# Up stores on ScalarE's and GpSimd's queues, fixed halo buffers, and a reordered beginning of the last projection in a hybrid decoder layer

## The chip, the cores and the metric

The kernel runs on one core of one Trainium2 chip. The metric is the device time in microseconds of one execution; the median of three runs of the kernel before is 2043.06 us (2043.0 to 2047.3). All arithmetic is float32; every matrix product is made of three passes (high part by high part, high by low, low by high), with a float32 split into a part that TensorE takes as it is (float32r) and the rest.

## The reference

One layer: a gated pair of token mixers, a projection with a layer norm, and then a gated feed-forward block with a three-tap causal convolution over time, again with a layer norm. The change touches the feed-forward block only (1024 positions, width 1024, hidden width 2816, so 5632 up columns):

```python
def conv_ffn(h, w_up, dw_w, dw_b, w_down):
    u = causal_dwconv(h @ w_up, dw_w, dw_b)
    gate, val = jnp.split(u, 2, axis=-1)
    return (jax.nn.silu(gate) * val) @ w_down

...
        ffn = conv_ffn(h, w_ffn_up[l], ffn_dw_w[l], ffn_dw_b[l], w_ffn_down[l])
        h = layer_norm(DN_ALPHA * h + ffn, ln2_g[l], ln2_b[l])
```

## The kernel before, in words

Both products of the feed-forward block are computed by a scheme of seven block products in place of eight: the operands are cut into 2 x 2 blocks, sums and differences of blocks are formed by VectorE, seven products are made, and their results are combined.

**Before the feed-forward block** (`ffn_blocks`, line 735): the normalised rows are transposed by TensorE, and the blocks b11, b21 (tile h1b1), b22, t1, t2 (tiles h1s) and t3, t4 (tile h1b2) are split into high and low parts. The pool of this stage is closed before the pool `up` opens, so that tiles of `up` stand in its memory.

**Up projection, first part** (`up_first`, line 806): for the first eight (`LEAD`) of 22 column blocks j the two products that need only b11 and b21 are made early, beside the transposing. ScalarE copies the bank (line 814), and a DMA on SyncE's queue (SP) stores the copy to `first_scr` (line 815).

**Up projection, rest** (`up_rest`, line 837): for each j, `up_weights` (line 817) loads two weight tiles `ra` (pool `wst`, tag `st`, three buffers, shared with all other weight loads) and `rb` (pool `up`, tag `raw`, three buffers), VectorE forms their sums (lines 828 to 831), and ScalarE and VectorE split them (lines 731, 732). TensorE makes five products (seven from j = 8 on) of 12 matmuls each. For j < 8 the early results are loaded back from `first_scr` (lines 859, 860). VectorE combines the banks into the gate and value columns `ug`, `uv` (lines 863 to 877), in three buffers of 1056 columns whose first two are zeroed by GpSimd (lines 846, 847), as the convolution reads two columns to the left. Then follow the three taps (line 883 on ScalarE, line 887 twice on VectorE), silu and the product (lines 897, 898), in three buffers `o`. Every second j belongs to the lower half of the hidden width; there VectorE forms the sums for the next scheme of seven (lines 912 to 915). All results go to HBM by DMAs on SP's queue: lines 908, 910, 916 and 917 (`b11_scr`, `b2_scr`, `t32_scr`, `t41_scr`).

**Last projection** (`down`, line 919): seven products p = 0 to 6, each of 11 steps k, a step being 12 matmuls. `load(p, k)` (line 952) fetches the step's block x of the hidden layer (line 968) and its weight blocks (lines 970 to 991) and splits them (lines 1006, 1007). Two sums of weight blocks are kept over several products: c3 (in a tile of the pool `big`, which has two buffers and holds h1b1 and h1b2 until the up projection has read them) and c4. In p = 0 the blocks a11 and a21 are loaded and c3 = a11 + a21 is formed; in p = 1, a12 and a22 and c4 = a12 + a22; p = 2 adds c3 to a22; p = 3 takes c3 and adds it to c4; p = 6 takes c4. The eight row tiles of the residual stream (`rows`, the other buffer of `big`) are loaded at the start (line 936). After each product VectorE adds its four banks to the rows (lines 1023 to 1054), and when a row tile is complete its layer norm is taken and it is stored.

**Order**: the functions are written in program order, and a scheduler orders the instructions of each engine by priority and a modelled time line when the program is built; `tc.high_priority(offset=n)` moves weight loads and their splits up. At run time each engine and each engine's DMA queue works strictly in the order that came out: an instruction that waits holds up all that stand behind it on its queue. Tiles in the same memory wait for each other's last readers.

Of the kernel before, what the change touches and what calls it, by code (L numbers as in the profile page):

```python
# [8 lines left out]
F32 = mybir.dt.float32  # L9
# [7 lines left out]
P = 128  # L17
# [39 lines left out]
def kernel(  # L57
# [748 lines left out]
    def up_first(fp, bl, j):  # L806


        w = weights(wup[2 * j], f"ue{j}")
        ps = bank(1)  # L810
        for q, block in enumerate(("b11", "b21")):
            product(ps, lambda i: w[:, i, q * HALF : (q + 1) * HALF], bl[block], q == 0)
            f = fp.tile([P, HALF], F32, tag="first", bufs=4, name=f"first{q}_{j}")
            A.copy(f, ps)
            SY.dma_start(first_scr[j][q], f)

    def up_weights(upp, j):


        with tc.high_priority(offset=2000):  # L820
            r1 = wst.tile([P, D], F32, tag="st", name=f"ra{j}")
            SY.dma_start(r1, wup[2 * j])
            r2 = upp.tile([P, D], F32, tag="raw", bufs=3, name=f"rb{j}")
            SY.dma_start(r2, wup[2 * j + 1])
            a11, a12, a21, a22 = r1[:, :HALF], r1[:, HALF:], r2[:, :HALF], r2[:, HALF:]
            ue = None if j < LEAD else split_pair(wsp, r1, f"ue{j}")
            s3 = upp.tile([P, HALF], F32, tag="s3", name=f"s3_{j}")
            V.tensor_tensor(out=s3, in0=a11, in1=a21, op=ALU.add)
            V.tensor_tensor(out=a21, in0=a21, in1=a22, op=ALU.add)
            V.tensor_tensor(out=a11, in0=a21, in1=a11, op=ALU.add)  # L830
            V.tensor_tensor(out=a12, in0=a12, in1=a11, op=ALU.add)
            w24 = split_pair(wsp, r1, f"s24_{j}")
            w10 = split_pair(wsp, r2, f"s10_{j}")
            w3 = split_pair(upp, s3, f"s3_{j}", HALF, 2)
        return ue, w24, w10, w3

    def up_rest(upp, bl, j, before):

        ue, w24, w10, w3 = up_weights(upp, j)
        ug, uv = (
            upp.tile([P, T + 32], F32, tag="u", bufs=3, name=f"f{n}{j}") for n in ("ug", "uv")
        )
        s = upp.tile([P, HALF], F32, tag="s", bufs=2, name=f"s{j}")
        G.memset(ug[:, :2], 0.0)
        G.memset(uv[:, :2], 0.0)
        early, late = slice(2, 2 + HALF), slice(2 + HALF, 2 + T)
        ps, pz = bank(1 if ue else 0), bank(0)
        if ue:  # L850
# [54 lines left out]
        )  # L905
        early, late = slice(0, HALF), slice(HALF, T)
        if j < NK:
            SY.dma_start(b11_scr[j], ov[:, early])
            return ov
        SY.dma_start(b2_scr[j - NK], ov)  # L910
        a, b, t = before, ov, og
        V.tensor_tensor(out=t[:, early], in0=a[:, late], in1=b[:, late], op=ALU.subtract)
        V.tensor_tensor(out=a[:, late], in0=a[:, early], in1=a[:, late], op=ALU.subtract)
        V.tensor_tensor(out=t[:, late], in0=t[:, early], in1=a[:, early], op=ALU.subtract)
        V.tensor_tensor(out=a[:, early], in0=b[:, early], in1=t[:, late], op=ALU.add)
        SY.dma_start(t32_scr[j - NK], t)
        SY.dma_start(t41_scr[j - NK], a)

    def down(upp, dp, g, b):

        LAST = 8
        X, Y = [bank(1) for _ in range(4)], [bank(0) for _ in range(4)]

        def flat_big(name):
# [5 lines left out]
        c4.append(upp.tile([P, HALF], F32, tag="s3", name="c4_last"))  # L932
        rs = [rows[:, t * D : (t + 1) * D] for t in range(8)]
        sts = [dp.tile([P, 2, 6], F32, name=f"st_f{t}") for t in range(8)]
        for t in range(8):
            SY.dma_start(rs[t], h1_scr[t * P : (t + 1) * P, :])
        E, L = slice(0, HALF), slice(HALF, D)

        def add(dst, x, y):
# [12 lines left out]
        def load(p, k):  # L952

            nonlocal n_steps
            a11, a21, a12, a22 = (wdown[h * NK + k, :, cs] for h in range(2) for cs in (E, L))
            x = (
                b11_scr[k],
                b2_scr[k][:, E],
                t32_scr[k][:, L],
                t32_scr[k][:, E],  # L960
                t41_scr[k][:, L],
                t41_scr[k][:, E],
                b2_scr[k][:, L],
            )[p]
            with tc.high_priority(offset=4000):
                st = raw("dr")
                w_st = st[:, E]
                SY.dma_start(st[:, L], x)
                if p == 0:
                    SY.dma_start(w_st, a11)  # L970
                    SY.dma_start(c3[k], a21)
                    add(c3[k], c3[k], w_st)
                elif p == 1:
                    SY.dma_start(w_st, a12)
                    SY.dma_start(c4[k], a22)
                    add(c4[k], c4[k], w_st)
                elif p == 2:
                    SY.dma_start(w_st, a22)
                    add(w_st, w_st, c3[k])
                elif p == 3:  # L980
                    w_st = c3[k]
                    add(c4[k], c4[k], c3[k])
                elif p == 4:
                    other = raw("do")[:, E]
                    SY.dma_start(w_st, a21)
                    SY.dma_start(other, a22)
                    add(w_st, w_st, other)
                elif p == 5:
                    SY.dma_start(w_st, a22)
                else:  # L990
                    w_st = c4[k]
                if p == 6 and k >= NK - 4:
                    if not last:
                        last.append(big_tile("last").rearrange("p i k t -> p (i k t)"))
                    w = last[0][:, (k - NK + 4) * 2 * D : (k - NK + 5) * 2 * D]
                    w = w.rearrange("p (i n) -> p i n", i=2)
                else:
                    own = n_steps % 2 and n_steps > 2
                    w = (dp if own else wsp).tile(
                        [P, 2, D], F32R, tag="w", bufs=3, name=f"w_dn{p}_{k}"  # L1000
                    )
                cuts = ((slice(0, D), st),) if w_st is not c3[k] and w_st is not c4[k] else (
                    (E, w_st), (L, st[:, L])
                )
                for cs, src in cuts:
                    A.copy(w[:, 0, cs], src)  # L1006
                    V.tensor_tensor(  # L1007
                        out=w[:, 1, cs], in0=src, in1=w[:, 0, cs].bitcast(F32), op=ALU.subtract
                    )
            n_steps += 1  # L1010
            return w
# [53 lines left out]
        for p, (banks, first, then) in enumerate(products):  # L1065
            end = NK - LAST if p == 6 else NK
            for k in range(end):
                w = load(p, k)
                for t in range(4):
                    block(banks[t], w, t, first, k)  # L1070
            ws = {k: load(p, k) for k in range(end, NK)}
            for t in range(4):
                for k in ws:
                    block(banks[t], ws[k], t, first, k)
                then(t)
# [26 lines left out]
    with pool("firsts", side="right") as fp:  # L1102
        for j in range(LEAD):
            up_first(fp, bl, j)
    upp = ctx.enter_context(pool("up"))
    before = None
    for j in range(NF):
        before = up_rest(upp, bl, j, before)
    ffn_stack.close()
    dp = ctx.enter_context(pool("down", side="right"))  # L1110
    g, b = row(dp, RW_2G, D, "ln2_g"), row(dp, RW_2B, D, "ln2_b")
# [100 lines left out]
```

## Time and profile before

| | |
|---|---|
| median of the runs | 2043.06 us |
| the profiled execution, first to last instruction | 2043.0 us |
| up_first ends (its last matmul) | 1402.5 us |
| up_rest, j = 0 to 7 | 1412.9 to about 1544 us |
| up_rest, j = 8 to 21 | to about 1816 us |
| last projection's matmuls | about 1805 to 2033.8 us |
| last layer norms and stores | to 2043.0 us |

The profile is of one execution. Times in it are counted from the first instruction. "PE" is TensorE's matmuls, "DVE" VectorE, "ACT" ScalarE, "POOL" GpSimd, "SP" SyncE, which issues all DMAs of this kernel; SPq marks its issues. "PEclk" or the granted clock is the share of full speed that TensorE was given. A row of a waits view reads: who waited, at which line, for which instruction; us in total, times, longest. A row of a time line reads: start, duration, engine, line, operation, output <- input, and in brackets the idle time before it and what ended it. In a chain view each row is a piece of the chain that ended last: start, duration, what.

### The profile page before, as it was taken

How to read it: one execution, taken by the hardware profiler on the slowest of the kernel's cores; microseconds unless marked ns; L12 is line 12 of the kernel's file. 1: busy time of each engine (PE TensorE's matmuls, PEld its weight loads, DVE VectorE, ACT ScalarE, POOL GpSimd, SP SyncE). 2: the span in 40 equal slices, each digit the busy share in tenths (PEclk: the TensorE clock that was granted, in tenths of full speed). 3: DMA queues.
4: the chain of work that ended last, by engine and by line, in shares of the span. 5: the costliest groups of instructions: out<-in, count | busy, mean ns of one | idle time of the engine just before them, and what ended most of it. 6: DMA issues, size and time to landing. Idle time of an engine off the chain costs nothing. (4 is left out here: it accounts for less than half of the span.)

```text
span 2043.0 us, 24683 instructions
## 1 busy us (share of the span) xinstructions
PE 1977.0 (97%) x9164; PEld 1627.7 (80%) x9164; DVE 1717.1 (84%) x2279; ACT 1001.3 (49%) x1431; POOL 146.8 (7%) x125
## 2 busy tenths in 40 slices
PE   7999999999999999999999999997899999989998
PEld 6888887888788888888888888876678888768886
DVE  7599999989766859999998976596888788789668
ACT  4465654556452356665454645453334445444432
POOL 2010101000400001010100040010000000000000
PEclk9999999999999999999999999998989999999999
DMA  6212223223436522222323253564343223287463
GB/s 218 93 68 89 87 93 103 98 103 114 160 124 218 200 93 73 93 78 87 117 88 109 107 175 127 207 234 174 124 138 119 95 98 117 101 316 267 145 226 109
DMA packets 99192, 275.10 MB, mean 135 GB/s; under 512 B 11264, under 2 KB 11264, under 8 KB 99072
## 3 DMA queue, kind: packets, MB, share of 16 engines
q1 hardware_dynamic: 99072, 273.52, 38.4%
q8 instruction: 72, 1.18, 0.2%
q14 instruction: 48, 0.39, 0.1%
HBM read 223.93 MB, written 49.55 MB: 134 GB/s over the span
## 5 line engine op out<-in xcount | busy, mean ns | idle before, releaser
L420 DVE SCALAR_TENSOR_TENSOR c<-v,pc,c 128x512 f32<-128x512 f32 x480 | 374.5, 803 | 7.7 <-ACT c L409 6.4
L478 POOL TENSOR_TENSOR au<-seg_mv,head_of 128x1024 fp32r<-128x1024 f32 x32 | 76.4, 2386 | 963.0 <-PE sm L487 730.1
L166 PE MATMUL acc<-hT,w_c 128*128 128x512 f32 x352 | 141.0, 401 | 0.0
L167 PE MATMUL acc<-hT,w_c 128*128 128x512 f32 x352 | 140.6, 399 | 0.0
L168 PE MATMUL acc<-hT,w_c 128*128 128x512 f32 x352 | 138.4, 393 | 0.0
L375 DVE SCALAR_TENSOR_TENSOR xbc<-u,pc,xbc 128x512 f32<-128x512 f32 x144 | 109.6, 773 | 0.7 <-ACT xbc L373 0.5
L1006 ACT CAST w_dn<-dr 128x1024 fp32r<-128x1024 f32 (+1 forms) x73 | 68.3, 944 | 76.6 <-PE sm L168 27.4
L167 PE MATMUL acc<-w_z,hT 128*128 128x512 f32 x256 | 100.8, 394 | 0.0
L166 PE MATMUL acc<-w_z,hT 128*128 128x512 f32 x256 | 100.8, 401 | 0.0
L168 PE MATMUL acc<-w_z,hT 128*128 128x512 f32 x256 | 100.7, 396 | 0.0
L154 ACT CAST w_c<-st_c 128x1024 fp32r<-128x1024 f32 x50 | 52.6, 1051 | 86.9 <-PE acc L168 66.2
L1007 DVE TENSOR_TENSOR w_dn<-dr,w_dn 128x1024 fp32r<-128x1024 f32 (+1 forms) x73 | 78.6, 1086 | 9.3 <-ACT w_dn L1006 9.1
L167 PEld LDWEIGHTS acc<-hT,w_c 128*128 128x128 f32 x352 | 66.1, 188 | 16.9 <-issue 3.8
L168 PEld LDWEIGHTS acc<-hT,w_c 128*128 128x128 f32 x352 | 66.1, 188 | 16.1 <-issue 2.6
L166 PEld LDWEIGHTS acc<-hT,w_c 128*128 128x128 f32 x352 | 66.1, 188 | 16.0 <-issue 2.6
L155 DVE TENSOR_TENSOR w_c<-st_c,w_c 128x1024 fp32r<-128x1024 f32 x47 | 60.5, 1287 | 20.3 <-ACT w_c L154 20.3
L166 PE MATMUL acc<-h1b,w_ue 128*128 128x512 f32 x176 | 68.8, 391 | 2.6 <-ACT w_ue L731 1.4
L731 ACT CAST w_s<-rb 128x1024 fp32r<-128x1024 f32 x22 | 23.2, 1053 | 94.7 <-PE sm L168 73.1
L166 PE MATMUL sm<-h1b,w_s 128*128 128x512 f32 x176 | 69.4, 395 | 0.0
L167 PE MATMUL sm<-h1b,w_s 128*128 128x512 f32 x176 | 69.2, 393 | 0.0
L168 PE MATMUL sm<-h1b,w_s 128*128 128x512 f32 x176 | 69.0, 392 | 0.0
L167 PE MATMUL acc<-h1b,w_ue 128*128 128x512 f32 x176 | 68.5, 389 | 0.0
(348 smaller groups left out, 5859.7 us busy)
## 6 DMA issues: line engine op xcount, KB each, us to landing
st_c<-wcol SPq DMA_DIRECT2D x50, 512.0 KB, 3.5
st_z<-wz SPq DMA_DIRECT2D x32, 512.0 KB, 3.5
dr<-wdown SPq DMA_DIRECT2D x55, 256.0 KB, 4.4
st_wo<-wo SPq DMA_DIRECT2D x24, 512.0 KB, 4.1
ra<-wup SPq DMA_DIRECT2D x22, 512.0 KB, 3.5
rb<-wup SPq DMA_DIRECT2D x22, 512.0 KB, 3.5
t_scr<-fo SPq DMA_DIRECT2D x22, 512.0 KB, 4.3
dr<-t_scr SPq DMA_DIRECT2D x44, 256.0 KB, 3.2
```

Source lines behind the costliest of these rows:

```text
L154: A.copy(w[:, 0, :], st)
L155: (eng or V).tensor_tensor(out=w[:, 1, :], in0=st, in1=w[:, 0, :].bitcast(F32), op=ALU.subtract)
L166: TE.matmul(ps, wa(0), xa(0), start=start, stop=False, skip_group_check=more)
L167: TE.matmul(ps, wa(0), xa(1), start=False, stop=False, skip_group_check=more)
L168: TE.matmul(ps, wa(1), xa(0), start=False, stop=stop, skip_group_check=more)
L375: V.scalar_tensor_tensor(out=o, in0=u[:, k : k + HALF], scalar=pc[:, wc + k : wc + k + 1], in1=o, op0=ALU.mult, op1=ALU.add,)
L420: V.scalar_tensor_tensor(out=accs[i], in0=v[:, k : k + HALF], scalar=pc[:, wc + k : wc + k + 1], in1=accs[i], op0=ALU.mult, op1=ALU.add,)
L478: G.tensor_tensor(out=au, in0=seg_mv[:, c, :].unsqueeze(1).to_broadcast([P, 8, P]), in1=head_of[:, g, :].unsqueeze(2).to_broadcast([P, 8, P]),
L731: A.copy(w[:, 0, :], src)
L1006: A.copy(w[:, 0, cs], src)
L1007: V.tensor_tensor(out=w[:, 1, cs], in0=src, in1=w[:, 0, cs].bitcast(F32), op=ALU.subtract)
```

## The change

In `up_first` the store is issued by ScalarE. In `up_weights` the second weight tile of j = 0 comes from the pool `wst`. In `up_rest` the columns lie in three buffers that are allocated once and whose first two columns are zeroed once, and the stores of the results are issued by GpSimd. In `down` the row loads go to GpSimd's queue, four after step 2 of product 0 and four after step 2 of product 2; product 0 loads only a11 (for the first five steps once into the staging tile and once, by GpSimd, into c3; from then on into c3 alone), product 1 loads only a12, into c4; product 2 loads a21 and a22 and forms c3 = a11 + a21, a22 + c3, and c4 = a12 + a22 + c3. From product 3 on the same sums are used.

```diff
@@ up_first
             A.copy(f, ps)
-            SY.dma_start(first_scr[j][q], f)
+            A.dma_start(first_scr[j][q], f)
@@ up_weights
-            r2 = upp.tile([P, D], F32, tag="raw", bufs=3, name=f"rb{j}")
+            if j:
+                r2 = upp.tile([P, D], F32, tag="raw", bufs=3, name=f"rb{j}")
+            else:
+                r2 = wst.tile([P, D], F32, tag="st", name=f"rb{j}")
@@ up_rest
-        ug, uv = (
-            upp.tile([P, T + 32], F32, tag="u", bufs=3, name=f"f{n}{j}") for n in ("ug", "uv")
-        )
+        ug, uv = us[2 * j % 3], us[(2 * j + 1) % 3]
-        G.memset(ug[:, :2], 0.0)
-        G.memset(uv[:, :2], 0.0)
...
-            SY.dma_start(b11_scr[j], ov[:, early])
+            G.dma_start(b11_scr[j], ov[:, early])
-        SY.dma_start(b2_scr[j - NK], ov)
+        G.dma_start(b2_scr[j - NK], ov)
...
-        SY.dma_start(t32_scr[j - NK], t)
-        SY.dma_start(t41_scr[j - NK], a)
+        G.dma_start(t32_scr[j - NK], t)
+        G.dma_start(t41_scr[j - NK], a)
@@ down
-        LAST = 8
+        LAST, EARLY = 8, 5
-        for t in range(8):
-            SY.dma_start(rs[t], h1_scr[t * P : (t + 1) * P, :])
+        def load_rows(ts):
+            for t in ts:
+                G.dma_start(rs[t], h1_scr[t * P : (t + 1) * P, :])
@@ load
-                if p == 0:
+                if p == 0 and k < EARLY:
                     SY.dma_start(w_st, a11)
-                    SY.dma_start(c3[k], a21)
-                    add(c3[k], c3[k], w_st)
+                    G.dma_start(c3[k], a11)
+                elif p == 0:
+                    w_st = c3[k]
+                    SY.dma_start(w_st, a11)
                 elif p == 1:
+                    w_st = c4[k]
                     SY.dma_start(w_st, a12)
-                    SY.dma_start(c4[k], a22)
+                elif p == 2:
+                    other = raw("do")[:, E]
+                    SY.dma_start(other, a21)
+                    SY.dma_start(w_st, a22)
+                    add(c3[k], c3[k], other)
+                    add(w_st, w_st, c3[k])
                     add(c4[k], c4[k], w_st)
-                elif p == 2:
-                    SY.dma_start(w_st, a22)
-                    add(w_st, w_st, c3[k])
                 elif p == 3:
                     w_st = c3[k]
-                    add(c4[k], c4[k], c3[k])
@@ the loop over products
                     block(banks[t], w, t, first, k)
+                if k == 2 and p in (0, 2):
+                    load_rows(range(2 * p, 2 * p + 4))
@@ before the loop over j
+    us = [upp.tile([P, T + 32], F32, name=f"u{i}") for i in range(3)]
+    for u in us:
+        G.memset(u[:, :2], 0.0)
...
-        before = up_rest(upp, bl, j, before)
+        before = up_rest(upp, us, bl, j, before)
```

More of the change, by code (lines that the diff above doesn't have):

```diff
@@ L835, in up_weights, with up_rest @@
         return ue, w24, w10, w3
-    def up_rest(upp, bl, j, before):
+    def up_rest(upp, us, bl, j, before):
         ue, w24, w10, w3 = up_weights(upp, j)
-        ug, uv = (
-            upp.tile([P, T + 32], F32, tag="u", bufs=3, name=f"f{n}{j}") for n in ("ug", "uv")
-        )
+        ug, uv = us[2 * j % 3], us[(2 * j + 1) % 3]
         s = upp.tile([P, HALF], F32, tag="s", bufs=2, name=f"s{j}")
-        G.memset(ug[:, :2], 0.0)
-        G.memset(uv[:, :2], 0.0)
         early, late = slice(2, 2 + HALF), slice(2 + HALF, 2 + T)
```

## The prediction

> **What bounds the kernel now.** I read the page first, then busy time by stage, then PE's waits, then the time line at each gap.
>
> ```profile
> PE 1977.0 (97%) x9164; PEld 1627.7 (80%) x9164; DVE 1717.1 (84%) x2279; ACT 1001.3 (49%) x1431; POOL 146.8 (7%) x125
> ```
>
> TensorE is the bound: 97% of the span of 2043.0 us. Only what it loses can be won, so the question is where the last third, the only part the diff touches, loses time. Busy time by stretches (PE, weight loads, DVE, ACT, POOL, then granted clock, DMA share, GB/s):
>
> ```profile
> 1402.50:1412.90 10.40, 0.41 (x3) 0.01 (x1) 4.98 (x9) 2.91 (x5) 0.00 (x0) 0.69 0.73 277
> 1412.90:1544.00 131.10, 118.17 (x482) 95.28 (x483) 114.04 (x140) 45.68 (x46) 1.21 (x12) 0.93 0.38 131
> 1544.00:1809.00 265.00, 263.30 (x1159) 216.82 (x1158) 216.44 (x245) 124.41 (x149) 2.92 (x29) 1.00 0.31 111
> 1809.00:1852.00 43.00, 35.36 (x141) 27.70 (x140) 36.82 (x42) 18.86 (x20) 0.00 (x0) 0.92 1.04 387
> 1852.00:2034.00 182.00, 181.83 (x803) 150.22 (x801) 144.72 (x207) 71.08 (x93) 0.00 (x0) 1.00 0.52 177
> ```
>
> There are three holes: at 1402, between 1413 and 1544, and between 1809 and 1852. The rest has none. PE's waits from 1402 on name them:
>
> ```profile
> PE sm L166 <- DVE fuv L869: 12.3, 3, 5.2
> PE sm L166 <- ACT w_s L731: 10.6, 2, 10.0
> PE acc L166 <- ACT w_dn L1006: 4.4, 1, 4.4
> PE acc L167 <- DVE w_dn L1007: 2.5, 2, 1.3
> ```
>
> A long wait costs a second time, because the clock falls. PE's time line, a steady stretch and the one behind the first hole:
>
> ```profile
> 1393.77 0.39 PE L166 MATMUL acc<-h1b,w_ue 128*128 128x512 f32 x1
> ...
> 1398.30 0.39 PE L168 MATMUL acc<-h1b,w_ue 128*128 128x512 f32 x1
> ...
> 1412.89 0.80 PE L166 MATMUL sm<-h1s,w_s 128*128 128x512 f32 x1 [9.99 <-ACT w_s L731]
> ...
> 1416.04 0.63 PE L168 MATMUL sm<-h1b,w_s 128*128 128x512 f32 x1
> ```
>
> Twenty starts lie between the first two rows: 4.53/20 = 0.227 us each. Between the last two lie seven: 3.15/7 = 0.45 us. **Hole A** (1402) is 10.0 us of idling; nine starts at the low clock, to 1416.8, lose some 9 x 0.21 = 1.9 us more: **11.9 us**. **Hole B**: the three waits on L869 are 12.3 us, and behind the two longest (5.2 and 4.5), from 1478.8 to 1484.9 and from 1513.7 to 1519.0, 14 and 12 starts at the same slow spacing lose 26 x 0.21 = 5.5 us: **17.8 us**. **Hole C**, the beginning of the last projection: 2.5 and 4.4 us of waits, and 12 slow starts behind the longer one, from 1837.8 to 1843.1, 2.5 us: **9.4 us**. Together 39 us; PE cannot get under about 2043 - 39 = 2004 by this change.
>
> **Part 1: the stores of up_first move from SP to ACT, and the second weight tile of j=0 to the staging pool.** SP's queue at hole A, and the DVE instruction it holds up:
>
> ```profile
> 1386.62 0.33 SPq L822 DMA_DIRECT2D ra<-wup  x1
> ...
> 1394.40 9.52 SPq L815 DMA_DIRECT2D first_scr<-first  x5
> 1403.97 1.39 SPq L824 DMA_DIRECT2D rb<-wup  x3
> 1407.89 0.69 DVE L828 TENSOR_TENSOR s<-ra,rb 128x512 f32<-128x512 f32 x1 [14.57 <-DMA rb<-wup]
> ```
>
> The last stores of up_first wait in SP's queue for ScalarE's copies of the last products. Behind them stand the first three rb loads, and DVE idles 14.6 us for them. The stores now stand behind their own copies on ACT, and rb0 no longer needs memory of the transposing stage: it takes the second staging buffer, which SP refilled at 1386.6 (now with ra1). With the 3.9 us that rb took from issue to use (1403.97 to 1407.89) it is there at about 1390.5. From L828 to the first matmul took 1412.89 - 1407.89 = 5.0 us. DVE is busy with the transposing stage until 1407.89 - 14.57 = 1393.3, so the first product is ready at about 1398.5, before PE's last matmul at 1402.5. The hole closes: **-11.9 us**. What hides the 4 us of spare time is up_first's last products; next late is w10, whose buffer only opens with the release of ue6, one product earlier.
>
> ACT pays for 16 issues:
>
> ```profile
> 1320.00:1402.50 82.50, 79.73 (x376) 65.45 (x375) 65.54 (x88) 49.34 (x78) 9.94 (x9) 1.00 0.63 229
> ```
>
> One issue takes 0.33 us on SP (L822 above), so by that some 16 x 0.33 = 5.3 us on ACT, which has 33 us idle in these 82.5. Hidden, 0; if that cover were gone, PE would wait 0.3 us per copy, since each second product adds onto the bank that ACT copies first.
>
> **Part 2: fixed halo buffers.** Gone are 44 two-column memsets (1.21 + 2.92 us of POOL above, on no chain); the three buffers rotate as before. 0.
>
> **Part 3: up_rest's stores move from SP to POOL.** Chain into the second L869 wait:
>
> ```profile
> 1469.14 5.80 DMA t_scr<-fo
> ...
> 1475.02 1.16 ACT fo L883
> ...
> 1478.14 0.61 DVE fuv L869
> 1478.79 0.80 PE sm L166
> ```
>
> and ScalarE's wait of this kind between 1395 and 1560 (us in total, times, longest):
>
> ```profile
> ACT fo L883 <- DMA t_scr<-fo: 5.3, 2, 2.9
> ```
>
> ScalarE waits until a conv buffer's store has landed, DVE's L887 waits for ScalarE, and L863 and L869, which PE needs, are queued behind it on DVE. SP issued that store as soon as it was ready, so SP's queue was not the trouble here, and the other queue gains nothing. What a store costs on POOL's queue no row shows, as before has no DMA from POOL. From below it is 0, or a little under, if POOL issues as promptly as SP (0.33 us); from above it is a POOL operation over a whole tile:
>
> ```profile
> L478 POOL TENSOR_TENSOR au<-seg_mv,head_of 128x1024 fp32r<-128x1024 f32 x32 | 76.4, 2386 | 963.0 <-PE sm L487 730.1
> 1384.22 1.29 POOL L785 TENSOR_TENSOR ts<-h1raw,ts 128x512 f32<-128x512 f32 x1 [4.63 <-DVE h1s L755]
> ```
>
> I take the shorter, 1.3 us, as nearer to an instruction that touches 128 rows but not all of their data. ScalarE waits for a store twice, each time ahead of one of the two long L869 waits: **+2.6 us** (0 to +4.8). The Trainium skill weighs in against this part: "SBUF — State Buffer", section "SBUF: two separate sides", says that a DMA from GpSimd has its descriptors written by GpSimd, and that a VectorE instruction in a 2-port mode can hold them up, 620 ns becoming 3100. By that rule at its worst the term would be an estimated 2 x 2.5 = 5.0 us; but the page gives those modes to copies, casts and tensor_scalar, and VectorE's operations in the chain above are none of these. No run here shows it yet.
>
> **DVE's lead.** With PE starting at 1402.5 DVE can have worked from 1393.3, 9 us, instead of 5 us as now. In 1412.9 to 1544 DVE worked 114 of 131 us, so it is nearly the bound there, and up to 4 us of lead can come off hole B. But the buffers of the split weights let it run ahead by little more than one step. I take half: **-2 us** (0 to -4).
>
> **Part 4: the last projection.** The chain into its long wait:
>
> ```profile
> 1830.06 6.54 DMA dr<-wdown
> 1836.69 1.05 ACT w_dn L1006
> ```
>
> After ScalarE's cast PE starts, at 1837.8. The block that ScalarE waits for (dr, a step of product one) is issued only at 1830, and takes 6.5 us. DMA is full here: 387 GB/s at a share of 1.04. Ahead of it in SP's queue, from 1796 to 1827, stand the eight row loads and the burst of blocks to be kept (c); the issues by size and median time to landing:
>
> ```profile
> c<-wdown SPq DMA_DIRECT2D x21, 256.0 KB, 5.4
> rows<-h_scr SPq DMA_DIRECT2D x8, 512.0 KB, 8.1
> ```
>
> So 22 of these 256 KB loads (one goes to the tile c_last), 5.8 MB. The first two products now take 22 x's, 22 blocks and 5 extra copies, 49 loads, instead of 66: 17 x 0.262 = 4.5 MB less. Four of the row tiles (2.1 MB) can come two products later. 6.6 MB at 387 GB/s are 17 us of DMA time, more than the hole. The 4.4 us wait and its slow clock go: **-6.9 us** (0 to -9.4). I leave the 2.5 us on DVE's L1007, where DVE still has the last blocks' conv to do.
>
> The 22 moved loads and adds fall in product three. DVE's groups there:
>
> ```profile
> L1007 DVE TENSOR_TENSOR w_dn<-dr,w_dn 128x1024 fp32r<-128x1024 f32 x20 | 24.0, 1213 | 0.8 <-ACT w_dn L1006 0.8
> L940 DVE TENSOR_TENSOR dr<-dr,c 128x512 f32<-128x512 f32 x11 | 7.3, 678 | 0.0
> L1027 DVE TENSOR_TENSOR rows<-rows,sm 128x512 f32<-128x512 f32 x4 | 2.6, 674 | 0.0
> L207 DVE BATCH_NORM_STATS2 st_f<-rows 128x6 f32<-128x512 f32 x4 | 2.5, 676 | 0.0
> ```
>
> Eleven steps of 1.21 + 3 x 0.68 = 3.25 us, plus 5.1 us at its start, are 41 us, against PE's 132 x 0.227 = 30.0. At most 11 us are missing, and the products on both sides have one split per step (13.3 us of 30), so DVE can run ahead there. A step takes two staging tiles of six, so its loads lead by three steps, 8.2 us, and the weights by up to six. I take 0, up to +3.
>
> **The sum**, against the profiled execution's 2043.0, which is its span and the lower end of the runs shown (median 2043.06): 2043.0 - 11.9 + 2.6 - 2.0 - 6.9 = 2024.8 us.
>
> **Rivals.** (1) *Hole B goes too.* Its waits come from an order on DVE, and the schedule of the whole up stage is made anew. If L863 and L869 stand ahead of the conv, all 17.8 us fall: 2043.0 - 11.9 - 17.8 - 6.9 = 2006. Against it: DVE's 114 of 131 us. (2) *Only one end wins.* The 11 blocks of product two (2.9 MB, 7.5 us at 387 GB/s) and the rows still burst ahead of the steps, or product three's DVE work takes back what product one gained: 2043.0 - 11.9 + 2.6 - 2.0 = 2031.7; with hole C closed and A not, 2038.7. (3) *No change.* The queues were not what was late: rb comes in time, but another part of step 0 (its s and ug from the first_scr stores, now ACT's) or the transposing stage's memory holds PE as long. Then 2043, within 4. The Trainium skill, "DMA: Bandwidth & Descriptors", section "Issuing engines are not separate DMA queues", has a rule to this effect: several issuing engines save only the time to initiate a DMA. By it only some 16 x 0.33 = 5.3 us of SP's issue time would be freed, none of it PE's; the 9.52 us row of L815 speaks against it, as that is waiting in order, not issue. (4) *Slower.* Late stores on POOL put more conv waits ahead of L863 and L869 in the first eight steps. Such a stall costs 5.2 + 14 x 0.21 = 8.1 us; two are there now. The other terms bring 11.9 + 2.0 + 6.9 = 20.8 us, so it decides from the third additional one on: three give 2043.0 - 20.8 + 24.3 = 2046, five 2063. For it: nothing but the buffers' number (three) covers a store; against it: only the odd steps store t tiles, and half of those four stall already. From step 8 on DVE has 48.6 us idle in 265 and would absorb it.
>
> **How the numbers follow.** Forecast, 2017 to 2032: 0.51. Rival 1, 2003 to 2017: 0.17. Rival 2, 2031 to 2039: 0.17. Rival 3: 0.06. Rival 4: 0.09. Predicted 2024.8. From 2004 to 2039 lie the forecast, rival 2 and most of rival 1, a little over 0.8; the bounds of the unknown costs, +2.2 for the stores, +2 for the lead, +6.9 for hole C and +3 for product three, end at 2024.8 + 14.1 = 2038.9. A change of 0.2%, 4 us, is about what a measurement of this kernel can tell from none: faster 0.85, within it 0.06, slower 0.09.
>
> **What would show it.** Step 1: rb0 issued near 1387, DVE's first L828 before 1396, no gap over 1 us at the switch to up_rest, granted clock 1.00 there. Step 3: t_scr's time to landing, and the L869 waits. Step 4: DMA share under 1 and no wait on L1006 at the start of the last projection; PE full through product three. I am wrong if PE still idles at the switch, if more than three waits on L869 are left, or if a new wait stands on L940.

## The result and the profile after

The changed kernel takes 2038.18 us (median of ten runs, 2035.64 to 2043.9), the kernel before 2044.17 us in ten runs beside it: a ratio of 0.9973, 95% interval 0.9963 to 0.9983, or some 5.5 us less. The forecast was 18.2 us less. The sign is right and the size is not. The profiled execution of the changed kernel is the slowest of its ten (span 2042.2 us); a second profile of the same kernel was taken with the experiments. The profile of the kernel before is of a run at the fast end of its own (2043.0 against a median of 2044.17), so the two profiles differ by less than the medians.

Busy time of the changed kernel by the stretches of its holes (PE, weight loads, DVE, ACT, POOL, granted clock, DMA share, GB/s); the stretches between them are full:

```profile
1402.50:1413.40 10.90, 5.60 (x14) 4.16 (x14) 8.38 (x11) 4.85 (x6) 0.00 (x0) 0.69 0.81 271
1413.40:1544.00 130.60, 120.22 (x500) 96.36 (x500) 116.05 (x142) 46.52 (x47) 7.16 (x13) 0.96 0.37 128
...
1804.20:1850.30 46.10, 37.15 (x138) 29.54 (x137) 30.97 (x37) 20.90 (x30) 6.41 (x12) 0.85 0.82 310
```

All three holes are still there: matmuls stand in 5.6 of 10.9 us at the first, and in 37 of 46 us at the beginning of the last projection, where the clock is now lower (0.85) than before (0.92). The four largest of PE's waits from 1380 on:

```profile
PE sm L166 <- DVE u L868: 9.2, 3, 3.9
PE sm L166 <- ACT w_s L731: 6.0, 2, 5.3
PE acc L166 <- ACT u L866: 5.7, 2, 5.4
PE acc L166 <- ACT w_dn L1012: 3.5, 1, 3.5
```

The longest wait for the split weights (A) is halved, from 10.0 to 5.3 us, and not gone; the waits behind the conv (B) are 3.1 us shorter, and the last projection has two waits of 5.4 and 3.5 us where it had one of 4.4 and two of 1.3.

To compare kernels I count at each hole what PE's starts lie further apart than the 0.227 us of a steady stretch, so the slow starts behind a wait count too. "Last matmul" is where PE's list ends.

| us lost by PE | A (switch, to 1428) | B (to 1535) | C (from 1787) | last matmul |
|---|---|---|---|---|
| before | 12.0 | 19.5 | 11.4 | 2033.4 |
| changed | 7.9 | 16.0 | 14.9 | 2032.1 |
| changed, second profile | 8.0 | 13.3 | 12.5 | 2028.7 |

So the changed kernel won 4 us at A and 3.5 to 6 at B, and gave 1 to 3.5 back at C, where 6.9 were to be won. B differs by 2.7 us between two profiles of the same kernel, so a difference of that size there says little.

**At A** the loads came as predicted: rb0 is issued at 1386.65 and VectorE's first sum runs at 1393.27. VectorE's and the chain's rows:

```profile
1393.27 0.68 DVE L831 TENSOR_TENSOR s<-ra,rb 128x512 f32<-128x512 f32 x1
...
1404.61 0.69 DVE L732 TENSOR_TENSOR w_s<-s,w_s 128x512 fp32r<-128x512 f32 x1 [9.93 <-ACT w_s L731]
```

```profile
1402.98 0.59 ACT first L814
...
1403.96 0.63 ACT w_s L731
...
1408.24 0.80 PE sm L166
```

The sum was ready at 1393.95 (1393.27 + 0.68); its high part is made only at 1403.96. ScalarE works in order, and the cast stands behind the copy of up_first's last product, which ends with up_first itself. VectorE idles 9.93 us for it. In the kernel before the order was the other way round; the same cast found ScalarE idle and waited 5.04 us for VectorE's sum:

```profile
1408.62 0.62 ACT L731 CAST w_s<-s 128x512 fp32r<-128x512 f32 x1 [5.04 <-DVE s L828]
```

rb0's new place also moved another load. The staging pool has three buffers. In before they hold ra0, ra1 and ra2; in the changed kernel rb0 takes one, and ra2 leaves SyncE 18.7 us later (first row before, second row changed; ra2 is the first of its three):

```profile
1391.36 0.33 SPq L822 DMA_DIRECT2D ra<-wup  x1
```

```profile
1410.08 3.27 SPq L822 DMA_DIRECT2D ra<-wup  x3
```

**At C** there are two bursts. GpSimd's time line at the first, and what ScalarE waits for:

```profile
1791.95 2.71 POOL L973 DMA_DIRECT2D c<-wdown  x5 [17.06 <-PE acc L168]
1794.65 0.54 POOL L909 DMA_DIRECT2D b_scr<-fo  x1
...
1818.90 4.25 POOL L937 DMA_DIRECT2D rows<-h_scr  x8 [5.18 <-PE sm L168]
```

```profile
1804.35 1.15 ACT L882 ACTIVATE fo<-u,pc 128x1024 f32<-128x1024 f32 x1 [3.91 <-DMA b_scr<-fo]
1807.30 1.15 ACT L882 ACTIVATE fo<-u,pc 128x1024 f32<-128x1024 f32 x1 [1.80 <-DMA t_scr<-fo]
...
1809.39 0.56 ACT L866 COPY u<-acc 128x512 f32<-128x512 f32 x1
```

When the memory of c3 opens near 1792, five of its blocks are issued by GpSimd and six by SyncE at once. Three stores of up_rest follow them. Their landings free the conv buffers: the first tap (L882) waits for the b_scr store, the second for a t_scr store, and the copy that PE waits for (L866) is queued on ScalarE behind both. The same kinds of store in a calm stretch (1544 to 1785) and here (1785 to 1806), by count, size and median us to landing:

```profile
t_scr<-fo POOLq DMA_DIRECT2D x12, 512.0 KB, 3.8
...
b_scr<-fo POOLq DMA_DIRECT2D x6, 512.0 KB, 2.9
```

```profile
t_scr<-fo POOLq DMA_DIRECT2D x2, 512.0 KB, 12.0
...
b_scr<-fo POOLq DMA_DIRECT2D x1, 512.0 KB, 9.6
```

The second burst: all eight row tiles go together at 1818.9, among ten blocks of c4 that SyncE issues from 1815.5 to 1822.4, though four of the rows were written two products later in the program. No data that these four need holds them back to that place, and the scheduler put them together. A block of the hidden layer pays, as the chain shows:

```profile
1827.19 16.75 DMA dr<-b_scr
...
1844.63 0.79 PE acc L166
```

### The profile page after: what moved, and what is told of

The parts are those of the page before. It is cut to its first block, busy times and chain, and to the rows that moved or that the text cites. A ratio compares the mean times of both kernels' runs of the same rounds, so it can differ in the third digit from the quotient of the medians.

```text
span 2042.2 us, 24581 instructions
## 1 busy us (share of the span) xinstructions
PE 1981.6 (97%) x9164; PEld 1630.7 (80%) x9164; DVE 1712.8 (84%) x2285; ACT 1001.6 (49%) x1448; POOL 173.1 (8%) x141
## 4 chain that ended last, share of the span: by engine, by line
PE 71%; DVE 20%; DMA 4%; issue 3%; ACT 1%; SPq 0%; POOL 0%; DVEq 0%; ACTq 0%; POOLq 0%
PE acc L166 18%; PE acc L168 18%; PE acc L167 18%; DVE c L420 6%; PE sm L166 4%; PE sm L167 4%; PE sm L168 3%; PE sm L534 2%; DMA dr<-b_scr 1%; PE acc L357 1%; DVE xbc L375 1%; DVE fo L886 1%; PE sm L515 1%; PE sm L192 1%; PE sm L523 1%
## 5 line engine op out<-in xcount | busy, mean ns | idle before, releaser
L886 DVE SCALAR_TENSOR_TENSOR fo<-u,pc,fo 128x1024 f32<-128x1024 f32 x88 | 111.6, 1280 | 10.2 <-ACT fo L882 9.7
L1012 ACT CAST w_dn<-dr 128x1024 fp32r<-128x1024 f32 (+1 forms) x73 | 60.8, 843 | 76.6 <-DVE dr L942 33.6
L1013 DVE TENSOR_TENSOR w_dn<-dr,w_dn 128x1024 fp32r<-128x1024 f32 (+1 forms) x73 | 69.8, 964 | 19.7 <-ACT w_dn L1012 19.5
L166 PE MATMUL acc<-h1s,w_s 128*128 128x512 f32 x168 | 66.8, 399 | 5.7 <-ACT u L866 5.7
L166 PE MATMUL acc<-h1b,w_ue 128*128 128x512 f32 x176 | 68.9, 392 | 2.6 <-ACT w_ue L731 1.4
```

What stands on the lines that cost most here:

```text
L166: TE.matmul(ps, wa(0), xa(0), start=start, stop=False, skip_group_check=more)
L886: V.scalar_tensor_tensor(out=o, in0=u[:, k : k + T], scalar=pc[:, wc + k : wc + k + 1], in1=o, op0=ALU.mult, op1=ALU.add,)
L1013: V.tensor_tensor(out=w[:, 1, cs], in0=src, in1=w[:, 0, cs].bitcast(F32), op=ALU.subtract)
```

## Experiments

Kernels that were run side by side on one chip share their runs of the kernel before; between groups I compare the ratios to before. The line numbers shift by a few between kernels.

### p1_first: before with part 1 alone

```diff
@@ before.up_first
-            SY.dma_start(first_scr[j][q], f)
+            A.dma_start(first_scr[j][q], f)
@@ before.up_weights
-            r2 = upp.tile([P, D], F32, tag="raw", bufs=3, name=f"rb{j}")
+            if j:
+                r2 = upp.tile([P, D], F32, tag="raw", bufs=3, name=f"rb{j}")
+            else:
+                r2 = wst.tile([P, D], F32, tag="st", name=f"rb{j}")
```

> Only part 1 (up_first's stores on ACT, rb0 in the staging pool), on the kernel before. Theory O (what is left of the hole at 1402 is ACT's order: the casts of step 0 stand behind the last copies of up_first on ACT): the hole goes from 12.0 us to about 8 as in the changed kernel, ACT's first cast of step 0 starts right behind the last first copy near 1403, and the time falls by 4 to 5 us, nearly all of what the whole change brought. Rival M (it is memory of the earlier pools that holds rb and the weights, and the store queue is no matter): hole at 12, within 2 us of before.

Measured: 2039.04 us, ratio 0.9968 (0.9956 to 0.998), all of the change's gain. Lost by PE: A 8.4, B 17.5, C 11.2. Its waits:

```profile
PE sm L166 <- DVE fuv L872: 10.2, 3, 4.7
PE sm L166 <- ACT w_s L731: 6.0, 2, 5.3
```

The wait on ScalarE's cast is the changed kernel's own 6.0. C, 11.2, is as before. B is 2 us less. VectorE's row behind its first two sums:

```profile
1405.30 0.69 DVE L732 TENSOR_TENSOR w_s<-s,w_s 128x512 fp32r<-128x512 f32 x1 [9.94 <-ACT w_s L731]
```

VectorE begins at 1393.95 and stands idle for 9.94 us of the time to PE's first product at 1408.93. That leaves it 5.0 us of work ahead of PE, as many as in before (1407.89 to 1412.89). So the 2 us at B are not a longer lead of VectorE; they lie within what two profiles of one kernel differ by.

### p3_stores: before with parts 2 and 3 alone

```diff
-            SY.dma_start(b11_scr[j], ov[:, early])
+            G.dma_start(b11_scr[j], ov[:, early])
...
+    us = [upp.tile([P, T + 32], F32, name=f"u{i}") for i in range(3)]
```

> Only parts 2 and 3 (fixed halo buffers, up_rest's stores on POOL). Theory O: a store on POOL lands as fast as one on SP (t_scr at 4.3 us median), the L869 waits stay at 12 us within 2, the time within 2 us of before. Rival S (POOL's stores are late by 1.3 us and more, as predicted): the two long L869 waits grow by 1.3 us each, time 2 to 5 us above before.

Measured: 2046.48 us, ratio 1.0005 (0.9996 to 1.0013): nothing. B loses 19.9 against 19.5. The landing times from 1380 to 1800, of before and of this kernel:

```profile
t_scr<-fo SPq DMA_DIRECT2D x18, 512.0 KB, 3.6
```

```profile
t_scr<-fo POOLq DMA_DIRECT2D x18, 512.0 KB, 4.1
```

A store by GpSimd takes 0.5 us longer to land and costs PE nothing that could be told.

### p4_down: before with part 4 alone, all up stores on SyncE

```diff
-        LAST = 8
+        LAST, EARLY = 8, 5
...
+                elif p == 0:
+                    w_st = c3[k]
+                    SY.dma_start(w_st, a11)
                 elif p == 1:
+                    w_st = c4[k]
                     SY.dma_start(w_st, a12)
```

(the whole of the change's edit of `down`)

> Only part 4 (the last projection), with up_rest's stores still on SP. Theory O (the loss at 1804 in the changed kernel is up_rest's last stores standing behind POOL's copies of c3, and the one at 1840 the eight rows all at once): no store stands behind POOL's copies here, so the hole at 1804 is under 3 us, and that near 1840 stays at 5 to 7; time 0 to 4 us under before. Rival D (the burst of c3 blocks fills DMA, whichever queue it is on, and the store lands late all the same): the hole at 1804 is there with 5 us and more, time 2 to 6 us above before. The prediction's own step (hole C closes): 7 us under before.

Measured: 2045.4 us, ratio 1.0006 (0.9994 to 1.0017). The profile is of its slowest run (2051.86). The hole at C is there without a store on GpSimd's queue. The chain:

```profile
1805.19 11.24 DMA b_scr<-fo
...
1816.54 1.16 ACT fo L883
```

The store is on SyncE's queue now and takes 11.24 us to land. So it is late on either queue; what stands ahead of it in both kernels are the eleven blocks of c3 (2.9 MB). That these are the cause is tested by x6_copies below. Part 4 wins nothing because it brings its own burst forward: in before the c blocks left SyncE from 1813 to 1827, as up_rest's last long stores landed (1815.3).

### x1_split0: the change, with the high parts of step 0 made by VectorE

```diff
@@ up_weights
+            hi = None if j else V.tensor_copy
-            w24 = split_pair(wsp, r1, f"s24_{j}")
+            w24 = split_pair(wsp, r1, f"s24_{j}", hi=hi)
```

(and so for w10 and w3)

> The changed kernel, but VectorE makes the high parts of step 0's three weight splits in place of ScalarE. Theory O: nothing of step 0 stands behind up_first's copies on ACT any more, the hole at 1402 goes from 7.9 us to under 1.5, granted clock 1.00 there, and the time falls by 5 to 8 us against the changed kernel (about 2031 to 2033 where the changed one is 2038). Rival V (VectorE bounds the first eight steps, so a start that is earlier is lost again in the L868 waits): the hole closes, but the L868 waits grow from 9.2 us to 14 and more, and the time is within 2 us of the changed kernel.

Measured: 2042.59 us, ratio 0.9985 (0.9975 to 0.9995), no better than the change. The hole at 1402 is gone, and one of 7.1 us stands at 1411. VectorE's row there:

```profile
1413.30 0.69 DVE L831 TENSOR_TENSOR s<-ra,rb 128x512 f32<-128x512 f32 x1 [5.82 <-DMA ra<-wup]
...
1414.64 1.22 DVE L732 TENSOR_TENSOR w_s<-ra,w_s 128x1024 fp32r<-128x1024 f32 x1
```

The first sum of step 2 (L831) stands ahead of the low part of step 1's w24 (L732) on VectorE, and waits for step 2's load ra2. ScalarE's cast was the first thing late at A; a load was the next. Closing the first alone won nothing: theory O fails, and PE's waits on L869 (8.3 us) did not grow as rival V has it.

### x5_first_pool: x1_split0, with up_first's stores on GpSimd

```diff
-            A.dma_start(first_scr[j][q], f)
+            G.dma_start(first_scr[j][q], f)
```

> The changed kernel with VectorE's high parts for step 0 as in x1_split0, and up_first's stores on POOL's queue in place of ACT's. In x1_split0 the hole went from 1402 to 1411, where ra2 on SP waited for the landing of the last store from ACT, whose completion count it shares. Theory L (it is this wait, so a store that shares no count with SP's loads ends it): hole at 1402 under 1 us, hole at 1411 to 1421 from 7.1 us to under 2.5, time 4 to 7 us under the changed kernel. Rival V (VectorE bounds the first eight steps): the L868 waits grow by what the start gains, time within 2 us of the changed kernel.

Measured: 2042.05 us, ratio 0.998 (0.9972 to 0.9989). A loses 7.5 us, now from 1414.8, so theory L fails. The same load is late, on SyncE's time line:

```profile
1393.89 13.32 SPq L827 DMA_DIRECT2D rb<-wup  x3
...
1408.93 0.48 SPq L860 DMA_DIRECT2D u<-first_scr  x1
1409.50 10.39 SPq L822 DMA_DIRECT2D ra<-wup  x3
```

ra2 is the first of the three in the last row. It no longer waits for the store's count; it leaves right behind the u load, and that stands behind the rb loads (x2567 below has the same order).

### after_again and x2_rows: the change, and the change with row tiles 4 to 7 tied to product two

```diff
@@ x2_rows, down
+                    if p:
+                        for t in range(4, 8):
+                            G.tensor_copy(rs[t][:, :1], w[:, 0, :1].bitcast(F32))
                     load_rows(range(2 * p, 2 * p + 4))
```

> The changed kernel once more, beside the three below: its time in the same company of runs, and whether its two holes in the last projection come again. All theories: 5 to 6.5 us under before (2038 to 2040 where before is 2044 to 2045); the hole near 1804 8 to 9 us, the one near 1840 somewhere from 3 to 7.

> The changed kernel, and GpSimd writes one column of row tiles 4 to 7 from the weights of step 2 of product 2 ahead of their loads, so that these loads can't go out before that step. Theory R (the hole near 1840 is the eight row tiles and the c4 blocks in DMA at once): 2.1 MB less there, 5.4 us at 390 GB/s, the wait on L1012 near 1840 and its slow clock go (6.4 us to under 2), the time 3 to 6 us under the changed kernel. Rival Q (it is SP's queue, whose next loads wait for staging tiles): the wait stays at 3 us and more, time within 2 us of the changed kernel.

Measured: the change again 2040.31 us, ratio 0.9974 (0.9962 to 0.9985); with late rows 2038.51 us, 0.9971 (0.9961 to 0.9981). The hole near 1840, 4.1 us in the second profile of the change, is closed, and a new one of 1.7 us stands at 1900. That is at most 2 us, and the intervals can't tell it from none. Theory R is right about the hole and wrong about the time.

### x6_copies: the change, with c3 and c4 filled by copies of the staged block

```diff
-        LAST, EARLY = 8, 5
+        LAST, EARLY = 8, NK
...
                     SY.dma_start(w_st, a11)
-                    G.dma_start(c3[k], a11)
+                    G.tensor_copy(c3[k], w_st)
...
-                    w_st = c4[k]
                     SY.dma_start(w_st, a12)
+                    G.tensor_copy(c4[k], w_st)
```

> The changed kernel, but c3 and c4 are not loaded beside the steps: each step's block goes to its staging tile, and GpSimd copies it on the chip into c3 (product 0) and c4 (product 1). 16 blocks that went out at once, as soon as their memory came free, now come one a step. Theory D (the burst fills DMA and makes the last stores of up_rest land late): the hole near 1804 goes from 8.5 us to under 2, the one near 1840 to under 3, the time 8 to 13 us under the changed kernel (about 2027 to 2031 where that is 2039). Rival P (what holds the stores is POOL's queue, in whose order the copies stand now): the hole at 1804 stays at 5 us and more.

Measured: 2028.67 us, ratio 0.9918 (0.9904 to 0.9932), 11.6 us under the change beside it. C falls from 12.5 to 1.5 us. The stretch in which the change had its two bursts, and all that PE waits for from 1780 on:

```profile
1804.20:1850.30 46.10, 46.10 (x203) 37.91 (x203) 40.44 (x36) 23.95 (x24) 27.18 (x29) 1.00 0.93 336
```

```profile
PE acc L166 <- ACT u L866: 1.2, 1, 1.2
```

GpSimd is busy for 27 us there, mostly with the copies. Each block now comes through a staging tile, so it can't be loaded before a tile is free: the loads come at the pace of the steps. The change's own loads into c3 and c4 (GpSimd's five, those into c3 from step 5 on, and those into c4) need no staging tile; the memory they go to opens at once, and so they all go at once. The b_scr store in 1785 to 1806 lands in 4.8 us in place of 9.6, the t_scr stores in 4.6 in place of 12.0. Five loads (1.3 MB) are gone as well, but DMA moves more in this stretch than in the change's (336 GB/s against 310) at a share of 0.93: it is the order of the bytes and not their number that was late. The eight row tiles still go together here, at 1810.0, and PE doesn't wait for them.

### x26: x6_copies and x2_rows together

```diff
+                    G.tensor_copy(c3[k], w_st)
...
+                            G.tensor_copy(rs[t][:, :1], w[:, 0, :1].bitcast(F32))
```

> The change with two edits: the blocks c3 and c4 are filled from the staging tile by GpSimd copies (no load of their own), and row tiles 4 to 7 wait for step 2 of product two. The copies alone gave 2028.7 and left no wait over 1.3 us in the last projection; the late rows alone gave 2038.5 and closed the hole near 1840. Theory D (the bytes of the burst are what is late, wherever they come from): with the c blocks gone the rows have room, nothing is left for the late rows to win: 2027 to 2030. Rival R (rows and stores still collide behind the averages): 1.5 to 3 us less, 2025.7 to 2027.

Measured: 2031.9 us, ratio 0.9934 (0.9921 to 0.9947). The time lies 2 us above both theories' ranges. C loses 1.5 us as with the copies alone, so the late rows have nothing left to win.

### x267: x26, and step 0's three and step 1's first high part by VectorE

```diff
+            hi = None if j else V.tensor_copy
...
-            w3 = split_pair(upp, s3, f"s3_{j}", HALF, 2)
+            w3 = split_pair(upp, s3, f"s3_{j}", HALF, 2, hi=V.tensor_copy if j < 2 else None)
```

> The edits of x26, and the high parts of step 0's three splits and of step 1's first one made by VectorE. With step 0's alone on VectorE the hole moved to 1411 to 1425 (7.1 and 7.5 us), where VectorE's low part of step 0's w10 stood behind step 1's w3, whose high part ScalarE made only after its last copy of up_first, and SyncE's load of ra2 waited for that low part. Theory A (in-order ScalarE is the whole of the hole): no gap over 2 us between 1395 and 1430, 5 to 8 us less than x26: 2020 to 2024. Rival B (VectorE is full from step 2 on, so what it wins at the switch it loses at its first combinations of the steps 2 to 6): the waits on L868 grow from 8.1 us to 12 or more, 2025 to 2028. Rival S (SyncE's wait for the first_scr stores is late next): a wait of over 4 us on a DMA of ra near 1412, 2027 to 2030.

Measured: 2026.66 us, ratio 0.9907 (0.9893 to 0.992), 5.2 us under x26 beside it; the profile is of its fastest run. A loses 7.2 us, B 12.1 (x26: 7.0 and 16.2), so by these profiles the gain is at B and ahead of the switch (up_first's last matmul starts 3.3 us sooner), not at A; its cause wasn't tried. The chain at A:

```profile
1400.90 5.73 DMA first_scr<-first
...
1406.69 4.02 DMA ra<-wup
```

ScalarE is off this chain, and the hole is as large as before: theory A falls, and rival S stands in the trace, though the time came out under its range. ra2 leaves as up_first's last store lands (1406.63). It needs nothing of that store. The trace's records name one completion semaphore, 104, for both, of the eight (101 to 108) that SyncE's and ScalarE's DMAs use in turn, and the new user waits for the last one.

### x2679: x267, with the fourth sum of steps 1 to 7 by GpSimd

```diff
-            V.tensor_tensor(out=a12, in0=a12, in1=a11, op=ALU.add)
+            (G if 0 < j < LEAD else V).tensor_tensor(out=a12, in0=a12, in1=a11, op=ALU.add)
```

> The edits of x267, and the fourth sum of the steps 1 to 7 (L834, 0.68 us on VectorE, six of them between 1430 and 1520) made by GpSimd, which is busy 5 of those 90 us and takes 1.6 us for a sum of this size. Theory F (the waits on L868 are VectorE's full queue: 84 of 90 us): they fall by up to 6 x 0.6 = 3.6 us against x267, 2 to 4 us less. Rival G (the later sum makes the weights late, or GpSimd slows VectorE): w24's low part waits for GpSimd, same as x267 or up to 5 us more.

Measured: 2030.06 us, ratio 0.9923 (0.9909 to 0.9937): 0.16% more than x267, about the size that can just be told. B loses 14.9 us against 12.1. GpSimd's sums take up to 2.2 us:

```profile
1457.06 2.21 POOL L834 TENSOR_TENSOR ra<-ra 128x512 f32<-128x512 f32 x1 [11.84 <-issue]
```

Theory F falls. Freeing VectorE of seven sums didn't shorten the waits behind the conv; why, beyond the later sum, wasn't tried.

### x2567: x267, with up_first's stores on GpSimd

> The edits of x267, and up_first's stores issued by GpSimd instead of ScalarE. In x267 ra2 was issued at 1406.69, as the last first_scr store of ScalarE's queue had landed (5.7 us after its issue), though ra2 has nothing to do with that store: in the build's order both wait on one completion semaphore of the hardware queues. Stores by GpSimd count on semaphores of their own. Theory M (the shared semaphore is what ra2 waits for): ra2 leaves right behind the last s and u loads of the steps 0 and 1, 3 to 4 us sooner, and the gap near 1410 (7.2 us lost) falls below 3 us: 2020 to 2023.5. Rival W (SyncE's queue is held by the rb loads ahead of it, which need the memory of up_first's last tiles, so it waits for those landings in any case, and GpSimd's stores land later): the gap stays at 5 us or more, 2025 to 2029. Rival B (VectorE takes it back): the gap falls, the waits on L869 grow from 8.7 us to 12 or more, 2025 to 2028.

Measured: 2028.07 us, ratio 0.9909 (0.9894 to 0.9924), as x267. The gap is 7.0 us. The chain of ra2:

```profile
1406.98 0.41 SPq L860
...
1407.49 6.85 DMA ra<-wup
```

The semaphore is no longer in the way (GpSimd's stores have 111 to 118): ra2 leaves 0.1 us behind the loads of s and u. But these stand behind rb2, which goes to memory of up_first's tiles and so waits for the landing of a store; SyncE comes free only at 1407.4, and sends ra2 behind six other loads of the last 3 us: 6.85 us to landing, 4.02 in x267. Rival W. Theory M was right in the trace and worth nothing in time.

### x2670 and x670: x267 with the one load ra2 on GpSimd, and the same without the late rows

```diff
-            SY.dma_start(r1, wup[2 * j])
+            (G if j == 2 else SY).dma_start(r1, wup[2 * j])
```

> The edits of x267 (up_first's stores by ScalarE again), and the load of ra2 alone issued by GpSimd. In the build's order ra2 needs the buffer of ra0, which VectorE's low part of step 0's w24 frees (1399.1 in x267); on SyncE it stands behind the rb and s loads and behind a completion semaphore that it shares with the last first_scr store (issued at 1406.69). Theory K (the place of ra2 in SyncE's queue is what is left of the hole): ra2 leaves near 1399 and lands before 1405, no gap over 2 us between 1395 and 1430, and the time falls by the gap's 5 to 7 us: 2019 to 2022. Rival B (VectorE's stretch from 1430 to 1520 is full, so a hole closed at the switch opens again at the first combinations): the waits on L869 grow from 8.7 us to 13 or more, 2024.5 to 2027. Rival W (rb2, which waits for the landing of a first_scr store in any case, comes next): a gap of 3 to 5 us stays, 2022 to 2025.

> The edits of x2670 without the late row tiles. The late rows won 1.8 us without the copies and nothing with them (2031.9 against 2028.7 for the copies alone, on other chips). If they are worth nothing beside the copies: within 1.5 us of x2670, either way. If the rows' share of the DMA still holds up the last projection: 2 to 4 us above x2670.

Measured: 2021.62 us, ratio 0.9891 (0.9876 to 0.9906), and 2020.28 us, 0.9881 (0.9864 to 0.9897). GpSimd's row of the load, the longest of PE's waits from 1380 on and the stretch of the switch, all of x670:

```profile
1404.13 0.73 POOL L822 DMA_DIRECT2D ra<-wup  x1 [17.75 <-DVE w_s L732]
```

```profile
PE sm L166 <- DVE u L869: 6.1, 2, 3.4
```

```profile
1390.00:1430.00 40.00, 36.93 (x158) 28.93 (x157) 29.49 (x43) 12.11 (x17) 0.73 (x1) 1.00 0.55 189
```

The load waits for its buffer alone (VectorE's L732 frees it) and for nobody's queue. The granted clock from 1390 to 1430 is 1.00, where x267 and the change have 0.91. A loses 2.7 us (x2670: 3.2), and B, 12.7 and 12.0, hasn't taken it back: theory K, in the hole and in the time. Its times for the load weren't met. VectorE still idles for ra2, less long (x267, then x670):

```profile
1410.79 0.69 DVE L831 TENSOR_TENSOR s<-ra,rb 128x512 f32<-128x512 f32 x1 [8.78 <-DMA ra<-wup]
```

```profile
1411.75 0.69 DVE L831 TENSOR_TENSOR s<-ra,rb 128x512 f32<-128x512 f32 x1 [4.99 <-DMA ra<-wup]
```

up_first's last matmul starts at 1399.9 in x267's profile and at 1403.3 in the other two. Counted from it the load lands after 10.9 us in x267, 6.1 in x2670 and 8.4 in x670. In the two new kernels VectorE's order changed a little too: L732, which PE waits for, stands right behind this L831, where x267 has another sum of 0.6 us between.

The single edit is the step from x267 to x2670: 4.0 us less at A, and a ratio of 0.9891 against 0.9907, 3.3 us, on another chip and with intervals that overlap. x670 and x2670 can't be told apart in time. x670 has the lowest median of all that was run, 0.9881 against the change's 0.9974, some 23 us under the kernel before beside it (2043.66 us).

| us lost by PE | A | B | C | ratio to before |
|---|---|---|---|---|
| p1_first | 8.4 | 17.5 | 11.2 | 0.9968 |
| p4_down | 13.6 | 21.7 | 12.6 | 1.0006 |
| x6_copies | 8.2 | 13.4 | 1.5 | 0.9918 |
| x267 | 7.2 | 12.1 | 1.5 | 0.9907 |
| x2670 | 3.2 | 12.0 | 1.5 | 0.9891 |
| x670 | 2.7 | 12.7 | 1.5 | 0.9881 |

## Why the prediction was right and wrong

**Part 1, -11.9: the step that failed is "the first product is ready at about 1398.5".** All before it came true: rb0 at 1386.65, the first sum at 1393.27. Then I moved the five microseconds from L828 to PE forward as one piece. In before that piece ran after up_first's end, so it held no wait for ScalarE, and it could not show one. Moved ahead of that end, it has ScalarE's casts in it, and these stand behind up_first's copies. The term came to -4.1. "Hidden, 0" for ScalarE's 16 issues asked the wrong question: not how busy ScalarE is, but what stands in its queue. "Next late is w10" was wrong too; step 1's w3 and step 2's load were next, and rb0's new place is part of that: with it a third tile sits in the three staging buffers, and ra2 has to wait for step 0's split. x670 shows that most of the term was there to be had: with the casts and ra2 out of these queues A loses 2.7, which is 9.3 under before's 12.0.

**Part 2, 0, and part 3, +2.6 (0 to +4.8):** p3_stores has them at 0 to the measurement's width. The store's price is 0.5 us to landing, not the 1.3 of a GpSimd operation, and the 0.54 us of issue falls on an idle engine. The Trainium skill's rule ("SBUF — State Buffer", section "SBUF: two separate sides", by which VectorE can hold up descriptors that GpSimd writes) would at its worst have shown as landings of an estimated 3.6 + 2.5 = 6.1 us; the 4.1 us row shows no such thing among VectorE's operations here.

**VectorE's lead, -2.0 (0 to -4):** p1_first has -2.0 at B, the changed kernel -3.5 and -6.2. The number agrees by luck, and the step failed with part 1's: "9 us, instead of 5 us" of work ahead of PE came to 5.0 in p1_first, as VectorE idled for ScalarE's cast. What made B smaller in the changed kernel stays open.

**Part 4, -6.9: came to +3.5 and +1.1.** Two steps failed. "Four of the row tiles (2.1 MB) can come two products later": they can, but nothing made them, and all eight went at 1818.9. And the sum of bytes (6.6 MB less, 17 us of DMA) treated the loads as if spread over the products. They are sent when their buffer opens, and the change gave eleven of them (c3) buffers that open at once and earlier, at 1791.7 where before's blocks left from 1813, and ten more (c4) at 1815.5. This second step is the one that cost the time: x2_rows mends the first and wins at most 2 us, and x6_copies, which gives the loads back their pace and leaves the rows together, closes C to 1.5 us. So the -6.9 was there to be had, by another edit.

**The rivals.** Nearest in kind was the second, by which blocks "and the rows still burst ahead of the steps"; but it meant the blocks of product two, where those of c3 and c4 burst, and it had A closed in full, and neither end was. Its other variant, C closed and A not, gives 2038.7, beside the measured 2038.2, and that is luck: A was closed by a third and C not at all. That an order on ScalarE would leave most of A open was in no case. The Trainium skill's rule behind rival 3 ("DMA: Bandwidth & Descriptors", section "Issuing engines are not separate DMA queues": other issuing engines save only the time of issuing) holds for the burst: the store takes 11.24 us on SyncE's queue and 9.6 on GpSimd's. It doesn't hold for the waits in order: moving the single load ra2, an issue of 0.33 us on SyncE, took PE's loss at A from 7.2 to 3.2 us.

**What stays open** is B: 12 to 13 us in the best version, behind VectorE's conv. Taking seven sums from VectorE didn't shorten it.

## What to carry to other kernels

When a stretch of work is moved forward past the end of a stage, its duration does not come with it: list for each of its instructions what stands ahead of it in its engine's queue and in its DMA queue at the new place, to the second and third step after it. A load is only as late as its gate: before counting bytes, find what opens each buffer, for loads that need no staging tile are sent in one burst and are paid for by a store or a small load that PE waits for. When a hole moves by some microseconds and keeps its size, the next thing late is already in the trace; follow its chain again before giving the hole up.

## What was not expected of the hardware

A 512 KB store takes 2.9 us to land in a calm stretch, 9.6 to 11.2 us beside eleven 256 KB loads issued just before it, on either queue. A load on SyncE waited 4.4 us (1402.3 to 1406.69 in x267) for another engine's store that shared its completion semaphore. Issuing a store costs GpSimd 0.54 us, and 0.33 on SyncE or ScalarE.
